# Attention layer on one core: the values' token sums on GpSimd, the products in another order, the heads' softmax apart, and another order at the end

## The chip, the cores and the metric

The kernel runs on one core of a Trainium2 chip. The metric is the device time of one launch in microseconds; the median of the runs shown is 1431.13 us (three runs, 1431.04 to 1432.65). One further execution was taken by the hardware profiler: it took 1434.23 us, of which the span of the instructions is 1432.5 us.

The engines are named as the profile names them: PE is TensorE (matmul; PEld its weight loads), DVE is VectorE, ACT is ScalarE, POOL is GpSimd, SP is SyncE, which here only issues DMAs.

## The reference, cut to what matters

Two layers on 512 tokens of width 1024, all in float32: a dilated window attention with 8 heads in three groups (windows 128, 512, 2048 with dilations 1, 4, 16), an mLSTM mixer, and a SwiGLU after each. Only the attention layer and the first lines of the SwiGLU behind it bear on the change:

```python
def dilated_attention_mixer(xn, positions, w_in, w_out):
    proj = (xn @ w_in).reshape(B, S, N_GROUPS, 3, ATTN_HEADS, ATTN_HEAD_DIM)
    ...
    for g, (window, dilation) in enumerate(DIL_CONFIGS):
        q = apply_partial_rope(proj[:, :, g, 0], positions) * scale
        k = apply_partial_rope(proj[:, :, g, 1], positions)
        v = proj[:, :, g, 2]
        o, lse = dilated_window_attention(q, k, v, window, dilation)
        ...
    wts = jax.nn.softmax(jnp.stack(lses), axis=0)
    o = jnp.einsum('gbsh,gbshd->bshd', wts.astype(xn.dtype), jnp.stack(outs))
    return o.reshape(B, S, ATTN_WIDTH) @ w_out

h = h + dilated_attention_mixer(rms_norm(h, attn_norm), ...)
h = h + swiglu(rms_norm(h, ffn_norm), ...)
```

## The kernel before, in words

**Split operands.** Each float32 operand of a matmul is split into a high half that TensorE takes exactly and the rest, the low half, and three matmuls are added: high times high, low times high, high times low. A chunk of weights (128 x 1024) comes by a DMA that SP issues (`load_chunk`, L201, three buffers), its high half is a copy on ScalarE (`split_chunk`, L209) and its low half a subtraction on DVE (L210). An operand is complete when L210 has run. Of the names, `a0g1k_k0` is the first half along the contraction of the weights for pair 0, group 1, keys; `_w`, `_h`, `_l` are the chunk and its halves. Activations are split in the same way (L224, L225; L228 where a gain is applied: `n_h`, `n_l`).

**Pairs of heads.** `project_pair` makes queries and keys of one pair of heads for the three groups, six projections of 48 matmuls. Each ends in one of three PSUM banks (`acc`); DVE multiplies it by the cosines out of the bank (L765 or L767) and shuffles the rotated part out (L556), after which the bank is free, then `rotate` finishes the rotation in SBUF (L559, L562, L564).

**Values.** For pair 0 the projections run beside the making of normalized tokens `xn` (`normalize`, L800: one DVE operation that multiplies h by the gain and by the broadcast inverse norm `xrbc`) and of four sums S1 to S4 of blocks of them (`sums_a`, `sums_b`, L830 to L839 with the splits L818 and L819). `values_phase` then makes the values of all heads with a Strassen scheme: seven products P1 to P7 for each of three units, with sums and differences of weight blocks made on DVE (L868) and split by L209 and L210. `prepare_values` runs two products ahead of `multiply_values`.

**Attention of a pair.** `attention_pair` makes scores (PE L633), their exponentials (DVE and ACT), and then `rest`: `joint` (the exchange between groups, PE L669), for each head `weigh` (DVE L701, L704) and `transposes` (a DVE transpose L710 to `pB` and four GpSimd-issued DMAs of it to DRAM, `pD`, L713), then for both heads `bring` (a GpSimd-issued DMA from `pD` into `pT`, L718). `values` multiplies `pT` with the values (PE L728, L733). `load_values` brings the values of a pair from DRAM (GpSimd-issued DMAs L595, L598).

**What sets the order.** The program is written out by hand and each engine takes its instructions in one order, which the scheduler derives from it and from what waits for what. `defer(n, fn)` puts work n steps (half projections) behind the present one, `advance` counts the steps, `run` closes a piece of PE work off by a fence, and `fenced` puts matmuls behind the last fence. The attention work of pair p runs so beside the projections of pair p + 1, at the steps of `RUN_AT`.

**The end.** The last pair has no projections beside it. The output projection (`awo`, four chunks of 256 columns, 24 matmuls for each half of the contraction) fills its place: `out_part(c, whl, ch, ks)` multiplies chunk c. Chunks 0 to 2 wait in PSUM for the last heads and are then added to h (L995); chunk 3 comes last, in one piece of 48 matmuls (`out_project(..., first=3)`). Then the squares of h are summed (`n1ssum`, L366) and the first SwiGLU starts with its weights `f0j`.

Of the kernel before, what the change touches and what calls it, by code (L numbers as in the profile page):

```python
# [17 lines left out]
P = 128  # L18
# [16 lines left out]
SCORES0_AT = 4  # L35
RUN_AT = (3, 5, 10)
STACK_AT = (9, 11, 15, 17)
# [34 lines left out]
def tile_hybrid_dilated_attn_mlstm(  # L72
# [296 lines left out]
    with ExitStack() as actx:  # L369
# [203 lines left out]
        def attention_pair(pr, qks):  # L573
# [13 lines left out]

            def load_values(last=False):
                for g in range(3):
                    t = (ap.tile([P, TB, 256], F32, tag="qk", name="%sv%d" % (nm, g), bufs=6) if last else  # L590
                         ap2.tile([P, TB, 256], F32, tag="v%d" % g, name="%sv%d" % (nm, g)))
                    src = vD[g][pr // 2][:, pr % 2 * 256:(pr % 2 + 1) * 256]
                    if g == 0:
                        for c in range(4):
                            nc.gpsimd.dma_start(t[R * c:R * (c + 1)],  # L595
                                                src.rearrange("(c b j) f -> c j b f", c=4, b=TB)[c])
# [151 lines left out]
            return (lambda: (places(), scores0(*qks[0])), lambda: scores12(*qks[1:]), rest, values, load_values)  # L748

        def project_pair(pr, qks, then=None):  # L750
# [3 lines left out]
            for g in range(3):  # L754
# [3 lines left out]
                for part in range(2):  # L758
# [26 lines left out]
                    if pr == 0 and 1 <= g and not first:  # L785
                        step = 2 * (g - 1) + part
                        (lambda: normalize(range(4)), lambda: normalize(range(4, 8)), sums_a, sums_b)[step]()
# [8 lines left out]
        def normalize(ks):  # L796
            for k in ks:
                if k % 2 == 0:
                    xn.append(place(("w2", "w3", "st0", "st1")[k // 2], "xn%d" % (k // 2)))
                nc.vector.scalar_tensor_tensor(xn[k // 2][:, k % 2], h[k], col("attn", k), rbc,  # L800
                                               op0=ALU.mult, op1=ALU.mult)

# [11 lines left out]

        def split_sum(name, raw):
            S[name] = ([heads_s[:, 2 * (int(name[1]) - 1) + i] for i in range(2)] if name in ("S1", "S2") else
                       [place("s%d" % (2 * (name == "S4") + i), name + "hl"[i], (P, 4, HALF), F32R) for i in range(2)])
            nc.scalar.activation(S[name][0], raw, AF.Copy)  # L818
            nc.vector.tensor_tensor(S[name][1], raw, S[name][0].bitcast(F32), op=ALU.subtract)  # L819
        sums = {}  # L820

        def two(fn):
            for i in range(2):
                fn(i, slice(2 * i, 2 * i + 2))

        def sums_a():
            nonlocal heads_s
            heads_s = ap.tile([P, 4, 4, HALF], F32R, tag="heads", name="S12")
            raw = sums["chain"] = place("w4", "Sr", (P, 4, HALF))
            two(lambda i, ks: nc.vector.tensor_tensor(raw[:, ks], xblock(1, 0, i), xblock(1, 1, i), op=ALU.add))  # L830
            split_sum("S1", raw)
            two(lambda i, ks: nc.vector.tensor_tensor(raw[:, ks], raw[:, ks], xblock(0, 0, i), op=ALU.subtract))
            split_sum("S2", raw)

        def sums_b():
            raw, r3 = sums["chain"], place("w5", "S3r", (P, 4, HALF))
            two(lambda i, ks: nc.vector.tensor_tensor(r3[:, ks], xblock(0, 0, i), xblock(1, 0, i), op=ALU.subtract))
            split_sum("S3", r3)
            two(lambda i, ks: nc.vector.tensor_tensor(raw[:, ks], xblock(0, 1, i), raw[:, ks], op=ALU.subtract))  # L839
            split_sum("S4", raw)  # L840
        heads_s = None
# [49 lines left out]
        def values_phase():  # L891
# [59 lines left out]
            for hf in range(2):  # L951
                load_block(0, "W12", hf)
            for hf in range(2):
                load_block(0, "W22", hf)
# [16 lines left out]
        def follow(todo, following=None):  # L971
            scores12_, rest, values, _ = todo[1:]

            def last():
                run(lambda: values(0), lambda: values(1))
                following[4]()
            defer(RUN_AT[0], lambda: run(scores12_))
            defer(RUN_AT[1], lambda: run(rest))
            if following is not None:
                defer(RUN_AT[2], last)  # L980
        for pr in range(1, HEADS // 2):
            qks = []
# [4 lines left out]
        _, last_scores, last_rest, last_values, load_last = todo  # L987
        out_first = split_chunk(weight_chunk(attn_w_out[0], 0, 0, 4, "awo0_k0"))
        pair = x_tiles("ao")
# [8 lines left out]
        def out_project(pairs, w2d, nk, name, first=0, end=KC // 2):  # L998
            for c in range(first, end):
# [3 lines left out]
        assert not later  # L1003
        acc = [[acc_tile("awo0_%d" % m) for m in range(2)],
               [ps.tile([P, 512], F32, tag="s", name="awo1_%d" % m, bufs=2) for m in range(2)],
               [acc_tile("awo2_0"), ps.tile([P, 512], F32, tag="t", name="awo2_1", bufs=1)]]

        def out_part(c, whl, ch, ks=None, last=False):
            for m in range(2):
                with fenced():  # L1010
                    multiply(acc[c][m], whl, pair, ch, m, KC, ks)
                if last:
                    add_to_h(c)(m, acc[c][m])

# [6 lines left out]
        load_last(True)  # L1021
        out_part(2, out_weights(2, 0), 0)
# [8 lines left out]
        for k in range(2, 4):  # L1031
            for c in range(3):
                out_part(c, whl[c], 1, (k,), k == 3)
# [1056 lines left out]
```

## Time and profile before

| | |
|---|---|
| median of three runs | 1431.13 us (1431.04 to 1432.65) |
| the profiled execution | 1434.23 us, span 1432.5 us |
| busy: PE, DVE, ACT, POOL | 97%, 80%, 50%, 11% of the span |
| mean granted clock of TensorE | 0.987 |
| attention layer, to the first matmul of f0j | 533.5 us |

The page cuts the span into forty slices of about 36 us, a digit each for the busy share in tenths; PE shows 9 in all slices but a few, and those are in the attention layer, at the start and at the end. In the list of waits each row names the engine and line that waited, what it waited for (engine or DMA, the tile and its line), the sum in us, the number of times and the longest. A row of the timeline holds the start, the duration, engine, line and operation, the tiles written and read, and in brackets how long the engine sat idle before it and what ended that.

### The profile page before, as it was taken

The page shows a single profiled execution, that of the slowest core. Times are in us where ns is not written, and L with a number is a line of the kernel's source. Part 1 is how long each engine was busy: PE and PEld are TensorE (multiplying, and loading weights), DVE is VectorE, ACT ScalarE, POOL GpSimd, SP SyncE. Part 2 cuts the span into 40 slices and gives each one's busy share as a digit, 9 for nine tenths or more (in the row PEclk, how much of TensorE's full clock was granted, in tenths as well). Part 3 has the DMA queues.
Part 4 walks back from the last instruction along what each step waited for, and adds up shares of the span by engine and source line. Part 5 has one row for each costly group of instructions (what it writes and reads, how often), then busy time and mean ns, then how long its engine had stood idle before and what let it go on. Part 6 is the DMA issues. An engine that isn't in the chain of part 4 may idle for free. (4 is left out here: it accounts for less than half of the span.)

```text
span 1432.5 us, 21509 instructions
## 1 busy us (share of the span) xinstructions
PE 1387.5 (97%) x8284; PEld 1233.9 (86%) x8284; DVE 1139.4 (80%) x1922; ACT 710.0 (50%) x1159; POOL 158.2 (11%) x229
## 2 busy tenths in 40 slices
PE   9889999999999699999999999999999999999997
PEld 7678888887877588999999998888888899999886
DVE  7997757768596559977887889988767987887887
ACT  6245544232232244444557654687444544557854
POOL 1000000201110101000001101022201240001203
PEclk9999999999999899999999999999999999999999
DMA  6425533726345426533335363323433563335963
GB/s 210 128 74 176 177 103 118 214 88 196 120 128 159 142 86 160 149 118 119 94 104 157 94 172 105 89 69 109 118 103 102 136 208 122 98 95 149 194 162 106
DMA packets 135231, 188.10 MB, mean 131 GB/s; under 512 B 8469, under 2 KB 100181, under 8 KB 135129
## 3 DMA queue, kind: packets, MB, share of 16 engines
q1 hardware_dynamic: 115136, 134.17, 30.2%
q0 software_dynamic: 18336, 51.43, 15.2%
q8 instruction: 65, 1.06, 0.3%
q10 hardware_dynamic: 1656, 1.12, 0.2%
q14 instruction: 38, 0.30, 0.1%
HBM read 164.68 MB, written 19.92 MB: 129 GB/s over the span
## 5 line engine op out<-in xcount | busy, mean ns | idle before, releaser
L1393 POOL DMA_DIRECT2D f1T<-in_ffn_w_out_dram x15 | 17.8, 1196 | 208.8 <-DMA f1P_2w_w<-in_ffn_w_out_dram 136.0
L1368 POOL DMA_DIRECT2D f0S<-in_ffn_w_out_dram x10 | 8.7, 894 | 247.4 <-DVE f0hid L1285 172.9
L1925 POOL DMA_DIRECT2D hD<-hB x32 | 21.7, 697 | 68.5 <-DVE hB L1922 68.5
L240 PE MATMUL awo<-ao_h,awo_k_h 128*128 128x512 f32 x64 | 25.9, 404 | 0.0
L240 PE MATMUL awo<-ao_h,awo_k_l 128*128 128x512 f32 x64 | 25.6, 403 | 0.2 <-DVE awo_k_l L210 0.2
L240 PE MATMUL awo<-ao_l,awo_k_h 128*128 128x512 f32 x64 | 25.6, 400 | 0.0
L240 PE MATMUL mo<-n_h,mo_k_l 128*128 128x512 f32 x64 | 25.3, 395 | 0.0
L240 PE MATMUL mo<-n_h,mo_k_h 128*128 128x512 f32 x64 | 25.2, 394 | 0.0
L240 PE MATMUL mo<-n_l,mo_k_h 128*128 128x512 f32 x64 | 25.1, 393 | 0.0
L240 PE MATMUL mwo<-yo_l,mwo_k_h 128*128 128x512 f32 x64 | 25.1, 393 | 0.0
L240 PE MATMUL mqk<-n_h,mqk_k_h 128*128 128x512 f32 x64 | 25.1, 392 | 0.0
L240 PE MATMUL mqk<-n_l,mqk_k_h 128*128 128x512 f32 x64 | 25.1, 392 | 0.0
L240 PE MATMUL f1j<-n_h,f1j_h 128*128 128x512 f32 x64 | 25.0, 391 | 0.0
L240 PE MATMUL f0j<-n_h,f0j_h 128*128 128x512 f32 x64 | 25.0, 391 | 0.0
L240 PE MATMUL mwo<-yo_h,mwo_k_l 128*128 128x512 f32 x64 | 25.0, 391 | 0.0
L240 PE MATMUL mqk<-n_h,mqk_k_l 128*128 128x512 f32 x64 | 25.0, 390 | 0.0
L240 PE MATMUL f0j<-n_h,f0j_l 128*128 128x512 f32 x64 | 24.9, 390 | 0.0
L240 PE MATMUL f1j<-n_h,f1j_l 128*128 128x512 f32 x64 | 24.9, 390 | 0.0
L240 PE MATMUL f0j<-n_l,f0j_h 128*128 128x512 f32 x64 | 24.9, 389 | 0.0
L240 PE MATMUL f1j<-n_l,f1j_h 128*128 128x512 f32 x64 | 24.9, 389 | 0.0
L240 PE MATMUL mwo<-yo_h,mwo_k_h 128*128 128x512 f32 x64 | 24.8, 391 | 0.0
L210 DVE TENSOR_TENSOR v1P_l<-v1W,v1P_h 128x1024 fp32r<-128x1024 f32 x14 | 17.1, 1224 | 9.5 <-ACT v1P_h L209 9.5
(2518 smaller groups left out, 5700.0 us busy)
## 6 DMA issues: line engine op xcount, KB each, us to landing
f0j_w<-in_ffn_w_in_dram SPq DMA_DIRECT2D x17, 512.0 KB, 5.7
f1j_w<-in_ffn_w_in_dram SPq DMA_DIRECT2D x17, 512.0 KB, 6.1
f1T<-in_ffn_w_out_dram POOLq DMA_DIRECT2D x15, 512.0 KB, 7.9
f0hid<-in_ffn_w_in_dram SPq DMA_DIRECT2D x9, 512.0 KB, 5.2
f1hid<-in_ffn_w_in_dram SPq DMA_DIRECT2D x9, 512.0 KB, 5.0
v0W<-in_attn_w_in_dram SPq DMA_DIRECT2D x8, 512.0 KB, 4.7
v1W<-in_attn_w_in_dram SPq DMA_DIRECT2D x8, 512.0 KB, 5.1
v2W<-in_attn_w_in_dram SPq DMA_DIRECT2D x8, 512.0 KB, 4.1
```

The lines of the kernel that those rows point to most:

```text
L210: nc.vector.tensor_tensor(lo[:, :n], raw[:, :n], hi[:, :n].bitcast(F32), op=ALU.subtract)
L240: nc.tensor.matmul(acc, whl[a][:, k, m * P:(m + 1) * P], pairs[b][kk], start=(kk == 0 and (a, b) == SPLITS[0]), stop=(kk == nk - 1 and (a, ...
L1368: nc.gpsimd.dma_start(t, src[1][:, ks], accum_op=ALU.add)
L1393: nc.gpsimd.dma_start(view(to), weight_rows(hk * UNITS + u, n), accum_op=ALU.add)
L1925: nc.gpsimd.dma_start(hD[k // 4].rearrange("(b i) x -> i b x", i=R)[:, :, c0:c0 + R], t[R * a_:R * (a_ + 1)])
```

## The change

- `normalize` becomes two operations: a scaled copy of h on ScalarE (L804) and a product with `xrbc` on GpSimd, in place (L805). All eight tokens' blocks are written in one step, where before there were two steps.
- The sums S1 to S4 are made on GpSimd (L828). The order is S1 and S3, then the split of S1, S2, the split of S3, the split of S2, S4, and the split of S4 in `values_phase`.
- The seven products run in the order P1, P5, P2, P6, P7, P3, P4.
- `rest` is cut in three: `joint` with the first head's weights and transposes; the first head's `bring` with the second head's weights and transposes; the second head's `bring`. They stand at steps 5, 7 and 9. The next pair's values are loaded group by group, at steps 10, 11 and 12.
- At the end the last scores come first, then the first halves of output chunks 0 and 3; chunk 3's first half is added to h at once. The three pieces of `rest` stand between the output chunks, whose parts come in another order, and of chunk 3 only the second half is left for the end.

```diff
-RUN_AT = (3, 5, 10)
+RUN_AT = (3, (5, 7, 9), 10, (10, 11, 12))
...
-            def rest():
+            def first_rest():
                 joint()
-                for i in range(2):
-                    weigh(i)
-                    transposes(i)
-                for i in range(2):
-                    bring(i)
+                weigh(0)
+                transposes(0)
+
+            def second_rest():
+                bring(0)
+                weigh(1)
+                transposes(1)
...
-                nc.vector.scalar_tensor_tensor(xn[k // 2][:, k % 2], h[k], col("attn", k), rbc,
-                                               op0=ALU.mult, op1=ALU.mult)
+                t = xn[k // 2][:, k % 2]
+                nc.scalar.activation(t, h[k], AF.Copy, scale=col("attn", k))
+                nc.gpsimd.tensor_tensor(t, t, rbc, op=ALU.mult)
...
+        def raw_sum(name, x, y, op):
...
+            for i in range(2):
+                nc.gpsimd.tensor_tensor(piece_of(name, i), piece_of(x, i), piece_of(y, i), op=op)
...
+        def raw_sums():
...
+            raw_sum("S1", of(1, 0), of(1, 1), ALU.add)
+            raw_sum("S3", of(0, 0), of(1, 0), ALU.subtract)
+
+        def more_sums():
+            split_sum("S1")
+            raw_sum("S2", "S1", of(0, 0), ALU.subtract)
+            split_sum("S3")
+
+        def last_sums():
+            split_sum("S2")
+            raw_sum("S4", of(0, 1), "S2", ALU.subtract)
...
-        ORDER = ("P1", "P5", "P6", "P2", "P7", "P3", "P4")
+        ORDER = ("P1", "P5", "P2", "P6", "P7", "P3", "P4")
...
         run(lambda: before[3](0, head_split), lambda: before[3](1, head_split))
-        out_part(0, out_first, 0)
         run(last_scores)
+        acc[0] = [acc_tile("awo0_%d" % m) for m in range(2)]
+        out_part(0, out_weights(0, 0), 0)
         load_last(True)
+        acc[3] = two_of("o", 3, 2)
+        whl = {3: out_weights(3, 0)}
+        for m in range(2):
...
+            add_part(3, m)
+        run(last_rest[0])
+        acc[1] = two_of("s", 1, 2)
+        out_part(1, out_weights(1, 0), 0)
+        last_rest[1]()
...
         out_part(2, out_weights(2, 0), 0)
-        run(last_rest)
-        out_part(1, out_weights(1, 0), 0)
         whl = [out_weights(c, 1) for c in range(3)]
-        for i in (0, 2):
-            out_part(i, whl[i], 1, (0, 1))
+        last_rest[2]()
+        for c in range(2):
+            out_part(c, whl[c], 1, (0, 1))
         run(lambda: last_values(0, head_split))
-        out_part(1, whl[1], 1, (0, 1))
+        out_part(2, whl[2], 1, (0, 1))
+        for c in range(2):
+            out_part(c, whl[c], 1, (2,))
         run(lambda: last_values(1, head_split))
...
-    out_project(pair, attn_w_out[0], KC, "awo", first=3)
+    whl = split_chunk(weight_chunk(attn_w_out[0], 1, 3 * 256, 4, "awo3_k1"))
+    for m in range(2):
...
+        add_to_h(3)(m, acc)
```

The change moves instructions at three places that the prediction speaks of. The first is DVE in pair 0, between the rotation of group 0 and the low half of the first key weights of group 1 (`a0g1k_k_l`); `xn_...` are normalized tokens. Before:

```order
L767 TENSOR_TENSOR a0g_q<-a0g1q_456,ropc 128x512
L556 STREAM_SHUFFLE rot<-a0g1q_456 32x512
L767 TENSOR_TENSOR a0g_q<-a0g1q_457,ropc 128x512
L556 STREAM_SHUFFLE rot<-a0g1q_457 32x512
L800 SCALAR_TENSOR_TENSOR xn_518<-h_97,cols,xrbc 128x512
L559 TENSOR_TENSOR rot<-rot,rops 32x1024
L800 SCALAR_TENSOR_TENSOR xn_521<-h_98,cols,xrbc 128x512
L564 TENSOR_TENSOR a0g_q<-a0g_q,rot 32x1024
L800 SCALAR_TENSOR_TENSOR xn_521<-h_99,cols,xrbc 128x512
L210 TENSOR_TENSOR a0g1k_k_l<-a0g1k_k_w,a0g1k_k_h 128x1024
```

The same place after the change:

```order
L770 TENSOR_TENSOR a0g_q<-a0g1q_456,ropc 128x512
L556 STREAM_SHUFFLE rot<-a0g1q_456 32x512
L210 TENSOR_TENSOR a0g1k_k_l<-a0g1k_k_w,a0g1k_k_h 128x1024
L770 TENSOR_TENSOR a0g_q<-a0g1q_457,ropc 128x512
L556 STREAM_SHUFFLE rot<-a0g1q_457 32x512
L129 COPY cols<-rowsT 128x72
L559 TENSOR_TENSOR rot<-rot,rops 32x1024
```

The low half now stands behind one evacuation and its shuffle instead of two, and the normalized tokens and the end of the rotation no longer stand ahead of it.

The second place is GpSimd's queue at the last pair, where `a3pD` are the transposed weights on their way to DRAM and `a3pT` the way back. Before:

```order
L598 DMA a3v_3611<-vD_376 128x4x256
L598 DMA a3v_3613<-vD_378 128x4x256
L713 DMA a3pD<-a3pB 32x4x480 x8
L718 DMA a3pT<-a3pD 128x1920 x2
L1368 DMA f0S_0_6339<-in_ffn_w_out_dram 128x512
```

After:

```order
L598 DMA a3v_3615<-vD_376 128x4x256
L598 DMA a3v_3617<-vD_378 128x4x256
L713 DMA a3pD<-a3pB 32x4x480 x5
L718 DMA a3pT<-a3pD 128x1920
L713 DMA a3pD<-a3pB 32x4x480 x3
L718 DMA a3pT<-a3pD 128x1920
```

The first head's way back now stands ahead of three of the second head's four ways out.

The third place is DVE at the change from the attention layer to the first SwiGLU, where `h_...` are the sums with the output chunks, `n1ssum` the sum of squares, `n_l_...` low halves of the scaled tokens and `f0j_00_l` the low half of the first SwiGLU weights. Before:

```order
L995 TENSOR_TENSOR h_101<-awo_1_3487,h_101 128x512
L366 TENSOR_TENSOR n1ssum<-n1ssum,n1sq 128x512
L210 TENSOR_TENSOR awo_k_l<-awo_k_w,awo_k_h 128x1024
L366 TENSOR_TENSOR n1ssum<-n1ssum,n1sq 128x512
L210 TENSOR_TENSOR f0j_00_l<-f0j_00_w,f0j_00_h 128x1024
L366 TENSOR_TENSOR n1ssum<-n1ssum,n1sq 128x512
L228 SCALAR_TENSOR_TENSOR n_l_3952<-h_96,cols,n_h_3951 128x512
L366 TENSOR_TENSOR n1ssum<-n1ssum,n1sq 128x512
```

After, the last rows of that stretch:

```order
L1009 TENSOR_TENSOR h_103<-awo_1_3943,h_103 128x512
L366 TENSOR_TENSOR n1ssum<-n1ssum,n1sq 128x512
L228 SCALAR_TENSOR_TENSOR n_l_3966<-h_98,cols,n_h_3965 128x512
L366 TENSOR_TENSOR n1ssum<-n1ssum,n1sq 128x512
L228 SCALAR_TENSOR_TENSOR n_l_3966<-h_99,cols,n_h_3965 128x512
L366 TENSOR_TENSOR n1ssum<-n1ssum,n1sq 128x512
L228 SCALAR_TENSOR_TENSOR n_l_3968<-h_100,cols,n_h_3967 128x512
L228 SCALAR_TENSOR_TENSOR n_l_3968<-h_101,cols,n_h_3967 128x512
L228 SCALAR_TENSOR_TENSOR n_l_3970<-h_102,cols,n_h_3969 128x512
L228 SCALAR_TENSOR_TENSOR n_l_3970<-h_103,cols,n_h_3969 128x512
L210 TENSOR_TENSOR f0j_00_l<-f0j_00_w,f0j_00_h 128x1024
```

The low half of f0j now stands behind all sums of h, all sums of squares and all eight low halves of the tokens; before, it stood behind the first six sums of h and two sums of squares.

More of the change, by code (lines that the diff above doesn't have):

```diff
@@ L586, in places, with load_values @@
                 p12.extend(t[:, 7:] for t in p)
-            def load_values(last=False):
-                for g in range(3):
+            def load_values(last=False, groups=range(3)):
+                for g in groups:
                     t = (ap.tile([P, TB, 256], F32, tag="qk", name="%sv%d" % (nm, g), bufs=6) if last else
@@ L816, in split_sum @@
+        def split_sum(name):
             S[name] = ([heads_s[:, 2 * (int(name[1]) - 1) + i] for i in range(2)] if name in ("S1", "S2") else
                        [place("s%d" % (2 * (name == "S4") + i), name + "hl"[i], (P, 4, HALF), F32R) for i in range(2)])
[L818 to L824, printed above, removed]
@@ L826, in sums_a @@
-        def sums_a():
+            hi, lo = S[name]
+            nc.scalar.activation(hi, raws_of[name], AF.Copy)
+            nc.vector.tensor_tensor(lo, raws_of[name], hi.bitcast(F32), op=ALU.subtract)
+        of = lambda t, kh: lambda i: xblock(t, kh, i)
+        def raw_sums():
             nonlocal heads_s
             heads_s = ap.tile([P, 4, 4, HALF], F32R, tag="heads", name="S12")
[L829 to L833, printed above, removed]
@@ L1003, in tile_hybrid_dilated_attn_mlstm, with out_part @@
         assert not later
[L1004 to L1008, printed above, removed]
+        two_of = lambda tag, c, bufs: [ps.tile([P, 512], F32, tag=tag, name="awo%d_%d" % (c, m), bufs=bufs)
+                                       for m in range(2)]
+        acc = {}
+        def out_part(c, whl, ch, ks=None, add=None):
             for m in range(2):
@@ L1011, in out_part, with add_part @@
                     multiply(acc[c][m], whl, pair, ch, m, KC, ks)
-                if last:
-                    add_to_h(c)(m, acc[c][m])
+                if add is not None:
+                    add(c, m)
+        def add_part(c, m):
+            add_to_h(c)(m, acc[c][m])
         def out_weights(c, ch):
@@ L1037, in tile_hybrid_dilated_attn_mlstm @@
         add_square(k)
-    out_project(pair, attn_w_out[0], KC, "awo", first=3)
+    whl = split_chunk(weight_chunk(attn_w_out[0], 1, 3 * 256, 4, "awo3_k1"))
+    for m in range(2):
+        acc = acc_tile("awo3_%d" % m)
+        with fenced():
+            for k in range(4):
+                for a, b in SPLITS:
+                    nc.tensor.matmul(acc, whl[a][:, k, m * P:(m + 1) * P], pair[b][4 + k],
+                                     start=(k == 0 and (a, b) == SPLITS[0]),
+                                     stop=(k == 3 and (a, b) == SPLITS[-1]))
+        add_to_h(3)(m, acc)
+    advance()
     for k in range(KC - 2, KC):
```

39 lines of the change are left out of this document (24 added, 15 removed).

## The prediction

> **What bounds the kernel now.** I read the page's busy shares first, then TensorE's waits, then tables of short windows around each wait, then the timeline there.
>
> ```profile
> PE 1387.5 (97%) x8284; PEld 1233.9 (86%) x8284; DVE 1139.4 (80%) x1922; ACT 710.0 (50%) x1159; POOL 158.2 (11%) x229
> PE a3o L728 <- DMA a3pT<-a3pD: 10.5, 1, 10.5
> PE a0g1k L240 <- DVE a0g1k_k_l L210: 4.6, 1, 4.6
> PE v0p L944 <- ACT v0P_h L209: 3.2, 1, 3.2
> PE a3g2k L240 <- DVE rot L556: 3.1, 1, 3.1
> PE a3xps L669 <- DVE a3ex L664: 2.2, 1, 2.2
> PE a1g2q L240 <- DVE a1g2q_k_l L210: 2.2, 1, 2.2
> ```
>
> TensorE is busy 1387.5 of 1432.5 us, so all its waits together are 45 us. The change leaves the number of matmuls as it is. It can therefore win only what these waits cost, and lose only by new ones; the largest six all lie in the attention layer, the first 533 us. A wait costs more than its length, as the windows show:
>
> ```profile
> 40.00:60.00 20.00, 14.95 (x58) 11.51 (x57) 19.54 (x29) 2.89 (x3) 0.00 (x0) 0.83 0.28 88
> 60.00:80.00 20.00, 20.00 (x90) 16.57 (x89) 19.43 (x28) 8.49 (x10) 0.00 (x0) 1.00 0.49 151
> 80.00:100.00 20.00, 15.74 (x61) 12.11 (x60) 20.00 (x26) 8.55 (x13) 0.00 (x0) 0.86 0.24 77
> ```
>
> The columns are busy time and count of PE, PEld, DVE, ACT and POOL, then the granted clock, the DMA share and GB/s. A full window holds 90 matmuls (0.222 us each). The first holds 58: 32 missing, 7.1 us, of which the wait at a0g1k is 4.6 and a small one 0.5. The other 2.0 us are matmuls at a low clock (0.83 in the mean) behind the wait. The third holds 61: 6.4 us lost, by the waits of 3.2 and 1.0 and again about 2 us of low clock. So I add 2 us to a wait of over 2 us. DVE is 97 to 100% busy from 40 to 100 us: there, what DVE does ahead of a needed operand sets the time.
>
> **1. The normalized tokens and their sums on GpSimd.** These are DVE's rows on the way to the first wait, then the wait:
>
> ```profile
> L800 DVE SCALAR_TENSOR_TENSOR xn<-h,cols,xrbc 128x512 f32<-128x512 f32 x8 | 5.6, 731 | 0.0
> L830 DVE TENSOR_TENSOR Sr<-xn,xn 128x512 f32<-128x512 f32 x2 | 1.3, 672 | 0.0
> 30.96 0.68 DVE L341 COPY xrbc<-xbc 128x512 f32<-128x512 f32 x1
> 39.47 2.33 DVE L559 TENSOR_TENSOR rot<-rot,rops 32x1024 f32<-32x1024 f32 x2
> 41.73 1.27 DVE L562 TENSOR_TENSOR a0g_q<-a0g_q,rot 32x512 f32<-32x512 f32 x2
> 42.93 1.28 DVE L562 TENSOR_TENSOR a0g_k<-a0g_k,rot 32x512 f32<-32x512 f32 x2
> 51.42 1.20 DVE L210 TENSOR_TENSOR a0g1k_k_l<-a0g1k_k_w,a0g1k_k_h 128x1024 fp32r<-128x1024 f32 x1
> 52.68 0.80 PE L240 MATMUL a0g1k<-xa_h,a0g1k_k_l 128*128 128x512 f32 x1 [4.57 <-DVE a0g1k_k_l L210]
> ```
>
> DVE loses eight products (5.6 us) and eight sums of two SBUF inputs (two in 1.3 us, so 0.6 to 0.67 each, about 4.9 us): 10.5 us. In the new order the low half of a0g1k also stands ahead of a second evacuation. If GpSimd cost DVE nothing, that L210 would end about 45.9 us (from 38.8, where the rotations then begin, one L800 of 0.7 before them being gone: four L562 and two L559 are 4.7, one evacuation with its shuffle 1.2, L210 1.2). The matmuls ahead of the wait end at 52.68 - 4.57 = 48.1, so it would be gone.
>
> Does GpSimd cost DVE nothing? At the end of the program stand four GpSimd products of the same form (128x512, two SBUF inputs):
>
> ```profile
> L1988 POOL TENSOR_TENSOR ht<-ht,gbc x4: 1300/1524/2347, 1413.0 to 1418.3; 128x512 f32<-128x512 f32 x4
> 1413.87 0.44 DVE L1993 TENSOR_TENSOR fpre<-fss 128x1 f32<-128x1 f32 x1
> 1414.23 1.21 DVE L210 TENSOR_TENSOR f1P_4w_l<-f1T,f1P_4w_h 128x1024 fp32r<-128x1024 f32 x1
> 1415.43 1.72 DVE L1339 TENSOR_TENSOR f1P<-f1hid,f1P 128x512 fp32r<-128x512 f32 x1
> L1339 DVE TENSOR_TENSOR f0P<-f0hid,f0P x25: 676/684/686, 745.3 to 858.3; 128x512 fp32r<-128x512 f32 x25
> ```
>
> The last row of the fence is not of this place, and shows what L1339 takes elsewhere: 0.68. Here, with GpSimd at work, it took 1.72, so 1.04 more. One GpSimd product takes 1.30 alone and 2.35 at worst, which is 1.05 more, about DVE's 1.2 of L210 that lay beside it. I read this as turns: a GpSimd product and a DVE operation with two SBUF inputs do not run at once, and neither gets two turns in a row.
>
> The Trainium skill ("SBUF — State Buffer", section "Who interferes with whom") calls these the shared pair of ports, held for a whole instruction, and lets a DVE instruction with one SBUF input pass; the rows agree with the holding. The Trainium skill ("GPSIMD Engine Reference", section 4.1) speaks against the move outright: element-wise work belongs on VectorE, GpSimd being some 2 times slower; 1.30 against 0.67 bears that out, and by it the move gains nothing.
>
> With turns: twelve GpSimd operations are ready from about 32 us, behind the copy of xrbc. Four or five of them pass beside DVE's evacuations from PSUM, to 38.8. Then stand six DVE operations with two SBUF inputs, and each waits for a GpSimd one: 4.7 + 5 x 1.30 + 0.4 = 11.6, to 50.4; evacuation and shuffle to 51.3 to 51.6, L210 to 52.5. Before it ended at 52.6. So the first wait stays: the 5.6 us taken off DVE are paid back in turns.
>
> Then the second place:
>
> ```profile
> 92.41 3.48 DVE L868 TENSOR_TENSOR v0W<-v0W,v0W 128x1024 f32<-128x1024 f32 x3
> 94.82 1.22 PE L944 MATMUL v0p<-v0P_h,S 128*128 128x512 f32 x2 [3.22 <-ACT v0P_h L209]
> 97.08 0.80 PE L944 MATMUL v0p<-v0P_l,S 128*128 128x512 f32 x1 [1.04 <-DVE v0P_l L210]
> ```
>
> P5 waits for the difference of weights (L868), which waits only for its turn on DVE. Taken off ahead of it: 10.5 us. Added: 6.9 in the turns above; for the five later GpSimd operations up to 1.30 each, taken at half, 3.3; and a new row of waits, about 1.5, since ScalarE's halves of the sums (S12, S3, S4) now wait for GpSimd, in a queue in which the halves of the weights a0g1k_k1, a0g2q and a0g2k stand behind them, and S4's low half on DVE waits for ScalarE. That is 11.7: P5 comes 1.2 later, say **+1.2 us**. Bounds: no turns, and both waits go with their low clock, 4.6 + 0.5 + 2.0 + 3.2 + 1.0 + 2.0 = 13.3 us faster; a full turn for each of the sixteen, 16 x 1.30 - 10.5 = 10.3 us slower. I stand near the middle because the rows at 1414 show turns, and because half of DVE's rows there read PSUM or have their operands apart. ScalarE's eight new scalings (about 0.6 each) lie in idle time: it is busy 2.89 us of 20 from 40 to 60.
>
> **2. P2 ahead of P6.** P2 needs no difference, so P6's is made behind it. TensorE has no wait at P6 that the list of before shows: 0, and at most 1.0, as at v0P_l, comes back.
>
> **3. The heads' softmax apart.** Pairs 1 to 3 wait at g2q for a low half (2.2 us in pair 1, no more in the others), with DVE full; the same work stands ahead of it in both orders, so these stay. The wait at a3g2k is of another kind:
>
> ```profile
> 418.00:430.00 12.00, 10.30 (x49) 8.41 (x48) 12.00 (x24) 3.56 (x9) 5.68 (x12) 1.00 0.90 246
> 430.00:442.00 12.00, 12.00 (x54) 9.68 (x52) 4.25 (x12) 2.73 (x11) 1.16 (x2) 1.00 0.97 289
> 427.65 0.55 POOL L718 DMA_DIRECT2D a2pT<-a2pD  x1 [4.01 <-DMA a2pD<-a2pB]
> 428.20 2.21 POOL L595 DMA_DIRECT2D a3v<-vD  x4
> 429.55 0.37 SPq L201 DMA_DIRECT2D a3g2k_k_w<-in_attn_w_in_dram  x1
> 441.65 1.06 ACT L209 ACTIVATE a3g2k_k_h<-a3g2k_k_w 128x1024 fp32r<-128x1024 f32 x1 [6.52 <-DMA a3g2k_k_w<-in_attn_w_in_dram]
> 445.26 0.50 PE L240 MATMUL a3g2k<-xa_h,a3g2k_k_h 128*128 128x512 f32 x1 [3.14 <-DVE rot L556]
> ```
>
> The weight chunk was issued at 429.55 and used at 441.65, 12.1 us on, with the DMA engines 0.90 to 0.97 busy: the second pT and four loads of values had been issued just ahead. Now the second head's transposes come about 3.5 us later, so these are issued behind the chunk. TensorE ran dry 3.1 us before 445.26; a chunk landing 3.1 us sooner ends the wait: **-5.1 us** (3.1 and 2.0 of low clock). Bounds: 0, if the pD traffic alone fills the engines; I take the full gain, since 12.1 us need only become 9.0. The second pT of pairs 0 to 2 lands later, but their products have 6 us to spare by my reading.
>
> **4. The end in another order.**
>
> ```profile
> 478.70 0.49 PE L669 MATMUL a3xps<-a3ex,acst 128*128 128x128 f32 x2 [2.17 <-DVE a3ex L664]
> 487.41 2.22 POOL L713 DMA_DIRECT2D a3pD<-a3pB  x4 [16.17 <-DVE a3pB L710]
> 494.61 0.56 POOL L718 DMA_DIRECT2D a3pT<-a3pD  x1
> 502.71 3.35 PE L728 MATMUL a3o<-a3pT,a3v 128*128 128x128 f32 x14 [10.49 <-DMA a3pT<-a3pD]
> 519.43 2.05 DVE L995 TENSOR_TENSOR h<-awo,h 128x512 f32<-128x512 f32 x3 [3.48 <-PE awo L240]
> 526.66 1.22 DVE L210 TENSOR_TENSOR f0j_l<-f0j_w,f0j_h 128x1024 fp32r<-128x1024 f32 x1
> 533.51 0.39 PE L240 MATMUL f0j<-n_h,f0j_h 128*128 128x512 f32 x1
> ```
>
> The scores now come first and 48 output matmuls (10.9 us) cover the softmax, so the wait at a3xps goes and the exchange comes 2.5 us sooner. The first pT now stands behind one pD of the second head instead of four, which is another 1.7 us at most: issue at 490.5 to 492 instead of 494.6. It landed 8.1 us on before; I take 5.5 to 8.1. So a3o starts between 496 and 500, at 498 say, **-4.7**, and TensorE waits some 5 us there.
>
> What follows has less cover. Of chunk 3's 48 matmuls 24 now stand ahead, so only 24 lie between the last sums of h and the first FFN. On DVE the low half of f0j's first weights, done by 527.9 (8.4 us after the first sum) before, now stands behind every sum of h, seven sums of squares and eight low halves of the normalized tokens. From the first sum: eight sums of h and seven of squares at 0.61, two L210 at 1.14, eight low halves at 0.66 (rows' durations less the 0.07 by which neighbours overlap: 526.66 + 1.22 ends at 527.9, and L800's form took 5.6 for eight): 9.2 + 2.3 + 5.3 = 16.8 us. TensorE comes to the first matmul that reads it 15 + 24 + 8 = 47 matmuls, 10.4 us, after the first sum, and waits about 6; with 2 of low clock it passes that point at 18.8. Before, the same point (f0j's ninth matmul, 8 x 0.222 past 533.51) lay at 15.9. That is **+2.9** against the -4.7: **-1.8 us**, from +0.6 (pT lands after 8.1) to -4.
>
> **Sum.** +1.2 + 0 - 5.1 - 1.8 = -5.7. The profiled execution took 1434.23 (span 1432.5 and 1.7 around it), so it would take 1428.5; the median of the runs shown is 1431.13, 3.1 below, and gives 1425.4. I round up to **1426**, as each step of 3 and 4 leans on a landing time.
>
> **Rivals.**
> (a) GpSimd and DVE hardly meet. For it: only eight DVE operations were beside GpSimd in the trace. Against: 1.72 for 0.68. Both early waits go: 1431.1 - 13.3 - 5.1 - 1.8 = 1411, and half of it 1419.
> (b) The moved traffic does not free the chunk. For it: the engines were 0.90 busy before pT too. Then 1426 + 5.1 = 1431, no change.
> (c) Slower: GpSimd becomes DVE's bottleneck between 32 and 92 us. Every one of sixteen operations holds DVE for 1.30, DVE comes 10.3 later to L868, and P5 waits 13 instead of 3: 1431.1 + 10.3 - 5.1 - 1.8 = 1434.5, and 1439.6 with (b). It decides from 13 full turns of the 16 on (17.4 us paid, 6.9 net, which eats what 3 and 4 bring). For it: DVE is 97 to 100% busy there, so every turn counts, and ScalarE's queue waits for GpSimd as well. Against: evacuations read PSUM. The Trainium skill ("GPSIMD Engine Reference", section 2.1) adds some 6 us at the first call of a freshly loaded GpSimd routine; no trace here shows that, and it would push the same way.
> (d) It does not do what it says: DVE gets its time back only to wait for GpSimd. That is my own step 1.
>
> **Chances.** Forecast 0.43 (own range 1421 to 1430), (a) 0.12, (b) 0.13, (c) 0.32. I give (c) this much because the two gains rest on landing times, while its cost lies on a full engine. A measurement of this kernel can tell about 0.2%, 2.9 us, from no change. Faster by more: 0.47 (eight tenths of the forecast's 0.43, and (a)); within: 0.2 ((b), the forecast's end); slower: 0.33 ((c), a little of (b)). Range: down to 1412, at the end of (a), and up to 1438, within (c) with (b).
>
> **What would show it.** Right: the wait at a0g1k still 3 to 5 us with L559 and L562 stretched by about 1.3 each beside GpSimd rows; P5 waiting 3 to 6; no wait at a3g2k nor a3xps; a3o waiting about 5; a new wait of about 6 at f0j's first matmul that reads a low half. Wrong: L562 at 0.6 beside GpSimd, and no wait at a0g1k (then (a)); a wait over 8 at P5 (then (c)); a chunk of a3g2k that takes 12 us again (then (b)).

## The result, and the profile after

The changed kernel takes 1432.57 us (median of 12 runs, 1430.48 to 1433.88), the kernel before 1431.09 us (12 runs, 1428.83 to 1433.71): a ratio of 1.0007, 95% interval 0.9999 to 1.0016. The forecast was 1426 us: no change was measured, where a gain of 5 us was the likeliest case. The profiled execution of the changed kernel took 1432.88 us, its span is 1431.1 us.

The page's busy shares, then TensorE's waits of the changed kernel (the total in us, times, the longest):

```profile
PE 1387.1 (97%) x8284; PEld 1234.1 (86%) x8284; DVE 1138.5 (80%) x1908; ACT 714.4 (50%) x1167; POOL 185.7 (13%) x245
PE a3o L728 <- DMA a3pT<-a3pD: 7.6, 1, 7.6
PE a0g1k L240 <- DVE rot L556: 5.2, 1, 5.2
PE v0p L956 <- ACT v0P_h L209: 3.8, 1, 3.8
PE f0j L240 <- DVE f0j_l L210: 2.7, 1, 2.7
PE n1ss L1102 <- DVE n1ssum L366: 2.4, 1, 2.4
PE a1g2q L240 <- DVE a1g2q_k_l L210: 2.2, 1, 2.2
...
PE a0g2k L240 <- DVE rot L556: 1.6, 1, 1.6
```

Two waits of before are not in this list any more, a3g2k (3.1) and a3xps (2.2). a3o is shorter by 2.9. Against that, a0g1k and P5 (v0p) are longer by 0.6 each, and three are new: two at the start of the first SwiGLU (5.1 together) and one at a0g2k. P5's second wait (1.0) is gone too, and one of 0.9 stands new at the product behind it. The sum of the waits hardly moved, and the time with it.

**Pair 0.** The timeline of DVE and the last rows of GpSimd's products there, with TensorE's wait:

```profile
38.75 4.58 DVE L559 TENSOR_TENSOR rot<-rot,rops 32x1024 f32<-32x1024 f32 x2
43.26 3.47 DVE L562 TENSOR_TENSOR a0g_q<-a0g_q,rot 32x512 f32<-32x512 f32 x2
46.66 3.41 DVE L562 TENSOR_TENSOR a0g_k<-a0g_k,rot 32x512 f32<-32x512 f32 x2
51.23 1.19 DVE L210 TENSOR_TENSOR a0g1k_k_l<-a0g1k_k_w,a0g1k_k_h 128x1024 fp32r<-128x1024 f32 x1
31.63 12.86 POOL L805 TENSOR_TENSOR xn<-xn,xrbc 128x512 f32<-128x512 f32 x8 [17.62 <-DVE xrbc L341]
44.44 3.41 POOL L828 TENSOR_TENSOR S1r<-xn,xn 128x512 f32<-128x512 f32 x2
51.37 0.79 PE L240 MATMUL a0g1k<-xa_h,a0g1k_k_h 128*128 128x512 f32 x1 [5.22 <-DVE rot L556]
52.48 0.80 PE L240 MATMUL a0g1k<-xa_h,a0g1k_k_l 128*128 128x512 f32 x1
```

The six operations L559 and L562 took 11.5 us, against 4.9 before: 6.6 more, 1.1 for each. GpSimd's sums take 1.70 each beside them instead of 1.30. These are the turns. The low half of a0g1k ends at 52.4, as forecast (52.5), and the wait stays. But it is not the low half that TensorE stops for first: the late evacuation holds a PSUM bank until its shuffle (L556) ends at 51.3, which before was done at 45.5. TensorE reads the low half at 52.48, before at 52.68.

Further on, DVE stands idle, which it did not before (rows of DVE with the idle time before them, one row of ScalarE, and P5):

```profile
59.96 1.23 DVE L210 TENSOR_TENSOR a0g2q_k_l<-a0g2q_k_w,a0g2q_k_h 128x1024 fp32r<-128x1024 f32 x1 [1.62 <-ACT a0g2q_k_h L209]
66.02 1.06 ACT L834 ACTIVATE S<-S1r 128x1024 fp32r<-128x1024 f32 x1 [6.09 <-POOL S1r L828]
68.06 1.23 DVE L210 TENSOR_TENSOR a0g2k_k_l<-a0g2k_k_w,a0g2k_k_h 128x1024 fp32r<-128x1024 f32 x1 [1.97 <-ACT a0g2k_k_h L209]
77.19 1.23 DVE L835 TENSOR_TENSOR S4l<-S1r,S4h 128x1024 fp32r<-128x1024 f32 x1 [2.28 <-ACT S4h L834]
97.38 1.22 PE L956 MATMUL v0p<-v0P_h,S 128*128 128x512 f32 x2 [3.78 <-ACT v0P_h L209]
```

DVE waits for ScalarE three times, 5.9 us of idle time on the engine that sets when P5 starts. Twice (1.97 and 2.28) ScalarE itself was held up by GpSimd's sums, for 6.09 and 5.29 us. The first time (1.62) it was not: the run below with the sums on DVE has 1.51 at the same place. P5 starts at 97.4 instead of 94.8, and the second unit of the values 2.6 us later than before (134.2, before 131.6).

**The last projection and the end.** Transfers and engines around a3g2k, then from the last pT to the first SwiGLU:

```profile
437.25 0.56 POOL L718 DMA_DIRECT2D a2pT<-a2pD  x1 [7.39 <-DMA a2pD<-a2pB]
432.20 0.37 SPq L201 DMA_DIRECT2D a3g2k_k_w<-in_attn_w_in_dram  x1
438.42 1.06 ACT L209 ACTIVATE a3g2k_k_h<-a3g2k_k_w 128x1024 fp32r<-128x1024 f32 x1 [0.64 <-DMA a3g2k_k_w<-in_attn_w_in_dram]
490.27 0.56 POOL L718 DMA_DIRECT2D a3pT<-a3pD  x1 [1.63 <-DMA a3pD<-a3pB]
498.26 3.33 PE L728 MATMUL a3o<-a3pT,a3v 128*128 128x128 f32 x14 [7.55 <-DMA a3pT<-a3pD]
515.33 2.06 DVE L1009 TENSOR_TENSOR h<-awo,h 128x512 f32<-128x512 f32 x3 [0.83 <-PE awo L240]
528.43 1.05 PE L1102 MATMUL n1ss<-ones,n1ssum 128*128 128x1 f32 x8 [2.39 <-DVE n1ssum L366]
530.95 2.35 DVE L210 TENSOR_TENSOR f0j_l<-f0j_w,f0j_h 128x1024 fp32r<-128x1024 f32 x2
532.21 0.79 PE L240 MATMUL f0j<-n_h,f0j_l 128*128 128x512 f32 x1 [2.73 <-DVE f0j_l L210]
```

The weight chunk of a3g2k is used 6.2 us after its issue (438.42 - 432.20), where before it took 12.1: the second pT and the values are issued behind it. From the start of the first sum of h to the first matmul that reads f0j's low half pass 16.9 us (532.21 - 515.33), as the sum of DVE's rows had it (16.8).

### The profile page after: what moved, and what is told of

It reads as the page before. It is cut to its first block, busy times and chain, and to the rows that moved or that the text cites. A ratio compares the mean times of both kernels' runs of the same rounds, so it can differ in the third digit from the quotient of the medians.

```text
span 1431.1 us, 21521 instructions
## 1 busy us (share of the span) xinstructions
PE 1387.1 (97%) x8284; PEld 1234.1 (86%) x8284; DVE 1138.5 (80%) x1908; ACT 714.4 (50%) x1167; POOL 185.7 (13%) x245
## 5 line engine op out<-in xcount | busy, mean ns | idle before, releaser
L210 DVE TENSOR_TENSOR v2P_l<-v2W,v2P_h 128x1024 fp32r<-128x1024 f32 x14 | 17.1, 1222 | 9.6 <-ACT v2P_h L209 9.6
L210 DVE TENSOR_TENSOR v1P_l<-v1W,v1P_h 128x1024 fp32r<-128x1024 f32 x14 | 17.1, 1223 | 9.6 <-ACT v1P_h L209 9.6
L210 DVE TENSOR_TENSOR v0P_l<-v0W,v0P_h 128x1024 fp32r<-128x1024 f32 x14 | 16.9, 1217 | 8.8 <-ACT v0P_h L209 8.8
L559 DVE TENSOR_TENSOR rot<-rot,sinn 32x1024 f32<-32x1024 f32 x18 | 21.7, 1207 | 0.1
```

Of the source, the lines that this page charges most:

```text
L210: nc.vector.tensor_tensor(lo[:, :n], raw[:, :n], hi[:, :n].bitcast(F32), op=ALU.subtract)
L559: nc.vector.tensor_tensor(sh, sh, sines.unsqueeze(1).to_broadcast([R, 2, SEQ]), op=ALU.mult)
```

## The experiments

The ratios are to the kernel before in the same session, since its median moves by 1 us from one session to the next (1431.09 to 1432.46). "v1c" is the start of the second unit of the values in the profiled execution, a point behind all the work of pair 0; before it lies at 131.6. It differs between traces of the same work: the three runs below with parts two to four and without the first have it at 130.7, 131.2 and 132.4.

**The four parts, each alone.**

Tokens and sums on GpSimd:

```diff
+                nc.scalar.activation(t, h[k], AF.Copy, scale=col("attn", k))
+                nc.gpsimd.tensor_tensor(t, t, rbc, op=ALU.mult)
...
+                nc.gpsimd.tensor_tensor(piece_of(name, i), piece_of(x, i), piece_of(y, i), op=op)
```

> The kernel before with only the first part of the change: normalized tokens and the four sums on GpSimd; products, softmax and end as before. My theory (turns on a shared way into SBUF): DVE's rows L559 and L562 between 38 and 50 us take about 1.1 us more each, the wait at a0g1k stays at 4 to 5.5 us, P5 starts about 2.5 us later than before (near 97.4 instead of 94.8), and the time is 2 to 3 us above before. Rival (the step relieves DVE, and what was lost was lost elsewhere): no change or faster, and P5 not later.

Measured: ratio 1.0017 (1.0008 to 1.0025), 2.4 us slower; v1c at 135.2; P5 at 98.1. L559 and L562 are as long as in the changed kernel. The first part costs time, by itself.

The softmax of the heads apart:

```diff
-RUN_AT = (3, 5, 10)
+RUN_AT = (3, (5, 7, 9), 10, (10, 11, 12))
```

> The kernel before with only the softmax of the two heads apart (steps 5, 7, 9, values group by group); the old tokens, products and end. My theory: the second chunk of a3g2k is issued ahead of the second pT, the wait of 3.1 us at a3g2k and its low clock go, 4 to 5 us faster. Rival: that wait is a matter of the one traced execution, the runs mostly don't have it, and the gain is 0 to 2 us. Second rival: the low clock that the wait at a1g2q then meets eats 1.6 us of it.

Measured: ratio 0.9964 (0.9952 to 0.9976), 5.1 us faster, with no wait at a3g2k. The first theory holds, but the size has two sources. The four other kernels that leave this part as it was show the wait at 1.3 to 2.8 us. From the first matmul of a3g0q to the first of a2o, a stretch with the wait in it, they and the kernel before take 75.8 to 79.3 us, 77.7 in the mean; this run takes 74.25. So 3.5 us come from there on average, and 5.0 only against the one trace of before. The rest comes at the last pair, whose `rest` is cut in three here too:

```profile
490.01 0.56 POOL L718 DMA_DIRECT2D a3pT<-a3pD  x1 [1.77 <-DMA a3pD<-a3pB]
```

Counted from the start of the last matmul of a2o, a3o starts after 39.5 us, in the five others after 40.5 to 41.1. The first pT was not issued sooner (33.0 us after that matmul, before 32.9), since it waits for its own pD; it landed after 6.3 us instead of 7.6 to 8.2.

The end in another order, with `rest` cut in its three pieces but run as one at step 5:

```diff
-            defer(RUN_AT[1], lambda: run(rest))
+            defer(RUN_AT[1], lambda: run(lambda: [fn() for fn in rest]))
...
(and the new end)
```

> The kernel before with only the new end of the attention layer. My theory: the wait at a3xps goes and a3o starts about 2 to 4 us sooner from the end of a2o, but the first SwiGLU waits about 5 us for n1ssum and f0j's low half; in sum between 1 us faster and 2 us slower. Rival (the end is worth what the prediction gave it): 2 us or more faster.

Measured: ratio 0.9989 (0.9978 to 1.0001), some 1.6 us faster, a little more than I expected at best. But the two parts are not apart in this run. GpSimd and ScalarE around a3g2k:

```profile
430.89 0.56 POOL L718 DMA_DIRECT2D a2pT<-a2pD  x1 [5.84 <-DMA a2pD<-a2pB]
434.80 1.04 ACT L209 ACTIVATE a3g2k_k_h<-a3g2k_k_w 128x1024 fp32r<-128x1024 f32 x1
```

The cut of `rest` alone puts the first head's `bring` ahead of the second head's transfers, so the second pT comes behind the weight chunk here too, and the wait at a3g2k is gone. The stretch from a3g0q to a2o takes 74.2 us here as well. This run holds the gain of the third part as well as the fourth. Behind it the new end is slower: from the last matmul of a2o to the first of the mLSTM 438.1 us, with the old end 437.1 to 437.6 in five traces. What the end is worth shows better between two kernels that both lack that wait, below.

The order of products:

```diff
-        ORDER = ("P1", "P5", "P6", "P2", "P7", "P3", "P4")
+        ORDER = ("P1", "P5", "P2", "P6", "P7", "P3", "P4")
```

> The kernel before with only the order of products P1, P5, P2, P6, P7, P3, P4. My theory: the wait of 1.0 us for P5's low half goes, the wait of 3.2 us for its high half stays; between 0 and 1.5 us faster. Rival: P2 only moves the same DVE work, no change at all at v1c's start (131.6 us).

Measured: ratio 0.9999 (0.9989 to 1.0009), v1c at 131.6 to the tenth. The rival holds: the wait of 1.0 us at P5's low half is gone, and a new one of 0.9 at the following product takes its place.

**Parts two to four without the first.** The tokens and sums as before, everything else as in the changed kernel:

```diff
-                nc.scalar.activation(t, h[k], AF.Copy, scale=col("attn", k))
-                nc.gpsimd.tensor_tensor(t, t, rbc, op=ALU.mult)
+                nc.vector.scalar_tensor_tensor(xn[k // 2][:, k % 2], h[k], col("attn", k), rbc,
+                                               op0=ALU.mult, op1=ALU.mult)
...
(and the sums on nc.vector)
```

> The changed kernel with tokens and sums as before, on DVE: parts two to four of the change without the first. My theory: the first part cost 2.6 us, so this is 2 to 3.5 us faster than the changed kernel and 1 to 4 us faster than before. Rival (GpSimd's share was free): as the changed kernel, within 1 us.

Measured: ratio 0.9979 (0.9969 to 0.9989), 3.0 us faster than before. Against the changed kernel's 1.0007 the first part costs about 4 us. Against the heads' softmax alone (0.9964) the new end and order cost 2.1 us by the ratios, but the two intervals overlap. The traces point the same way: from the last matmul of a2o to the first of the mLSTM it is 435.5 us with the old end and the heads apart (457.0 to 892.5) and 437.7 with the new one (455.8 to 893.5). So the end as it stands brings nothing, and is likely a loss.

**f0j's low half.** The first weights of the SwiGLU are split ahead of the normalized tokens in program order:

```diff
+    early = [split_chunk(weight_chunk(ffn_w_in[0], 0, half * D_FF, 4, "f0j0_%d0" % half)) for half in range(1)]
     pair, rbc, _, hook = norm("ffn", 0, "n1", ssum)
```

> The changed kernel with f0j's first weights split ahead of the normalized tokens, so that their low half stands behind one sum of squares on DVE. My theory: the waits of 2.4 and 2.7 us at the start of the first SwiGLU and the low clock behind them go for the larger part, 3 to 6 us faster than the changed kernel. Rival (DVE's chain of sums and low halves is itself the bound, whatever stands first): under 1.5 us faster, with the wait now at a low half of the tokens.

Measured: ratio 0.9951 (0.9935 to 0.9966), 7 us faster than before, and by the two ratios 8 us faster than the changed kernel. The timeline of DVE, and TensorE's first matmul that reads the low half:

```profile
513.46 2.06 DVE L1009 TENSOR_TENSOR h<-awo,h 128x512 f32<-128x512 f32 x3 [0.82 <-PE awo L240]
518.95 1.22 DVE L210 TENSOR_TENSOR f0j_l<-f0j_w,f0j_h 128x1024 fp32r<-128x1024 f32 x1
523.03 0.39 PE L240 MATMUL f0j<-n_h,f0j_l 128*128 128x512 f32 x1
```

The gain is larger than the 3 to 6 us that I expected. The low half is done 6.7 us after the start of the first sum of h instead of 16.8, TensorE reads it without a wait, and the low clock behind the two waits goes too. From f0j's first matmul to the first of the mLSTM it is 366.3 us (522.1 to 888.4) instead of 373.3. The same 24 matmuls of chunk 3 are enough cover, if that one row stands early. So the place in DVE's order was the cause, not the length of its chain.

Both of the last two:

```diff
(parts two to four of the change, and the early split; tokens and sums on nc.vector)
```

> Both: tokens and sums on DVE as before, and f0j's first weights split early. If the two losses are independent, 5 to 9 us faster than the changed kernel, 4 to 8 faster than before (1423 to 1427 us). If they are not, no more than the better of the two alone.

Measured: 1422.19 us, ratio 0.9931 (0.9916 to 0.9946), 9.9 us faster than before, more than the 4 to 8 expected. Against the changed kernel that is 10.9 us by the ratios, and the two runs before give 4 and 8: the two losses add up within the noise, and this version beats both kernels. TensorE's waits in it:

```profile
PE a3o L728 <- DMA a3pT<-a3pD: 6.9, 1, 6.9
PE a0g1k L240 <- DVE a0g1k_k_l L210: 4.6, 1, 4.6
PE v0p L947 <- ACT v0P_h L209: 3.2, 1, 3.2
```

**What GpSimd costs DVE.** Two constant writes in place of each of the sixteen GpSimd operations; this leaves the products and the sums of the tokens out.

```diff
-                nc.gpsimd.tensor_tensor(t, t, rbc, op=ALU.mult)
+                nc.gpsimd.memset(t, 1.0)
+                nc.gpsimd.memset(t, 1.0)
...
(the same for the sums)
```

> The changed kernel with each of the sixteen GpSimd operations replaced by two writes of a constant to the same place (about 1.1 us together), which read nothing from SBUF; so the products and sums of the tokens are left out. My theory (what costs DVE its time is GpSimd's reading beside it): L559 and L562 go back to 1.13 and 0.6 us, the wait at a0g1k is under 1 us, P5 starts without a wait of over 1.5 us, and it is 8 to 14 us faster than the changed kernel. Rival (any GpSimd work on SBUF holds DVE): L562 still near 1.7 us each and no more than 4 us faster.

Measured: ratio 0.9961 (0.9946 to 0.9976). DVE's rows in the run in which GpSimd writes and does not read:

```profile
45.35 2.33 DVE L559 TENSOR_TENSOR rot<-rot,rops 32x1024 f32<-32x1024 f32 x2
47.61 1.27 DVE L562 TENSOR_TENSOR a0g_q<-a0g_q,rot 32x512 f32<-32x512 f32 x2
```

They are back at 1.2 and 0.6 each, and 0.3 is left of the wait at a0g1k. But GpSimd was done with the first writes by 43 us, before L559 began, so this run shows what the absence of GpSimd's work is worth and not that a writing GpSimd beside these rows would be harmless. The gain is smaller than I expected: 6.6 us from the changed kernel by the ratios, not 8 to 14. P5 still waits 1.7, and a new wait of 3.1 stands at a0g0q, for a high half on ScalarE, whose order moved.

**Tokens or sums?** Only the eight token products on GpSimd, the sums on DVE; and the other way round:

```diff
(first) +                nc.gpsimd.tensor_tensor(t, t, rbc, op=ALU.mult)
(second) +                nc.gpsimd.tensor_tensor(piece_of(name, i), piece_of(x, i), piece_of(y, i), op=op)
```

> The kernel before with only the eight token products on ScalarE and GpSimd; the four sums stay on DVE. It parts the 2.4 us that the first part costs. My theory: the turns (L559 and L562 are 6.6 us longer together) about pay for the 5.6 us taken off DVE, the rest of the loss is DVE idle behind sums made on GpSimd; so here v1c starts within 1.5 us of the kernel before (131.6), and P5 within 1.5 of 94.8. Rival (the turns are the whole loss): v1c 2.5 us or more later.

> The kernel before with only the four sums on GpSimd; the token products stay on DVE. My theory: DVE loses some 5 us of sums and gains 4 to 6 us of idle time, since ScalarE's halves of the weights stand behind its halves of the sums and those wait for GpSimd; v1c starts 1 to 3 us later than before. Rival (the loss is all in the turns with the token products): v1c at 131.6 or earlier.

Measured: tokens alone 0.9990 (0.9978 to 1.0003), v1c at 130.6; sums alone 1.0029 (1.0017 to 1.0041), v1c at 135.3, which is 3.7 us later and more than the 1 to 3 expected. The loss is in the sums. (With the sums the order of their splits moves too, as in the change; that order with the sums on DVE was not run.) The tokens alone, timeline:

```profile
31.94 11.29 POOL L802 TENSOR_TENSOR xn<-xn,xrbc 128x512 f32<-128x512 f32 x8 [17.55 <-ACT xn L801]
35.33 1.77 DVE L838 TENSOR_TENSOR S3r<-xn 128x512 f32<-128x512 f32 x1 [1.25 <-POOL xn L802]
45.37 1.28 DVE L562 TENSOR_TENSOR a0g_q<-a0g_q,rot 32x512 f32<-32x512 f32 x2
93.45 0.94 PE L945 MATMUL v0p<-v0P_h,S 128*128 128x512 f32 x2 [4.03 <-ACT v0P_h L209]
```

GpSimd is done at 43.2, before L562 begins, and most of its work lay beside DVE's evacuations. So the turns that I had put down to the tokens come for the larger part from the sums that follow them. Of the wait at a0g1k 1.1 us are left instead of 4.6, but 1.5 stand new at a0g1q, for an evacuation behind a sum on DVE that itself waits for a token (the second row). And at v1c 1 us arrives, which is no more than the spread of that point: DVE stays 100% busy from 60 to 100 us, and P5 now waits 4.0 and 1.3. The wait moved along the queue of the full engine.

The sums alone, timeline:

```profile
57.44 5.91 POOL L824 TENSOR_TENSOR S1r<-xn,xn 128x512 f32<-128x512 f32 x2 [2.48 <-DVE xn L800]
58.61 1.21 DVE L210 TENSOR_TENSOR a0g2q_k_l<-a0g2q_k_w,a0g2q_k_h 128x1024 fp32r<-128x1024 f32 x1
59.75 1.20 DVE L831 TENSOR_TENSOR S3l<-S3r,S3h 128x1024 fp32r<-128x1024 f32 x1
63.38 1.06 ACT L830 ACTIVATE S<-S1r 128x1024 fp32r<-128x1024 f32 x1 [7.33 <-POOL S1r L824]
64.35 1.04 ACT L209 ACTIVATE a0g2q_k_h<-a0g2q_k_w 128x1024 fp32r<-128x1024 f32 x1
64.48 1.23 DVE L831 TENSOR_TENSOR S<-S1r,S 128x1024 fp32r<-128x1024 f32 x1 [3.52 <-ACT S L830]
```

Two sums take 5.9 us on GpSimd. ScalarE waits 7.3 us for them with the high half of a0g2q queued behind, and DVE waits 3.5 us for ScalarE. DVE was freed of these sums and stood idle for them. The two sums are not alike:

```profile
L824 POOL TENSOR_TENSOR S1r<-xn,xn x2: 1282/2977/4672, 57.4 to 62.1; 128x512 f32<-128x512 f32 x2
```

The first took 4.67 us, until 1.2 us after the last DVE row had ended at 60.95, and the DVE rows beside it kept their usual length; the second took 1.28 beside an idle DVE. So here GpSimd did not get every other turn: several DVE rows passed before it.

**What a3o waits for.** The last pair's transfers from ScalarE's queue, on top of the best version:

```diff
-                    nc.gpsimd.dma_start(d.rearrange("b j a x -> a j b x")[a],
+                    (nc.scalar if pr == HEADS // 2 - 1 else nc.gpsimd).dma_start(d.rearrange("b j a x -> a j b x")[a],
...
(the same for pT)
```

> Tokens and sums on DVE, f0j's first weights split early, and the last pair's pD and pT transfers issued from ScalarE's queue instead of GpSimd's (ScalarE is busy 2 of 20 us there). It parts what a3o waits for. If the issue of 0.55 us each on GpSimd and its descriptors are what is late, a3o's wait of 6.9 us falls by 2 to 4 us, to 1418 to 1420 us. If the transfers' own time on the DMA engines is (8 us from issue to use), it stays within 1 us of 1422.

Measured: 1422.53 us, ratio 0.9931 (0.9915 to 0.9947), no change. The issue of the first pT and the start of a3o, first from ScalarE's queue, then from GpSimd's (the best version):

```profile
487.32 0.35 ACTq L718 DMA_DIRECT2D a3pT<-a3pD  x1
495.96 3.33 PE L728 MATMUL a3o<-a3pT,a3v 128*128 128x128 f32 x14 [7.06 <-DMA a3pT<-a3pD]
486.98 0.56 POOL L718 DMA_DIRECT2D a3pT<-a3pD  x1 [1.51 <-DMA a3pD<-a3pB]
494.38 3.33 PE L728 MATMUL a3o<-a3pT,a3v 128*128 128x128 f32 x14 [6.86 <-DMA a3pT<-a3pD]
```

From the start of the last matmul of a2o the pT is issued after 29.8 us here and after 30.8 from GpSimd. It is used 8.6 us later instead of 7.4, so that a3o starts after 38.4 and 38.2 us. The issue came 1.0 us sooner and the use did not. So the queue that issues them is not what a3o waits for; what is left is the transfers themselves, to DRAM and back. What sets their length was not tested.

## Why the prediction was right or wrong

The measured time lies inside the range, at the case "no change" (0.2) rather than the forecast (0.43). That it does is owed to a range that reaches up to 1438: the gain of 5 us did not come. Point by point, in the terms of the sum:

- **Step 1, forecast +1.2; measured +2.4 (1.1 to 3.6) alone, about 4 within the change.** The mechanism was right: turns, the wait at a0g1k stays, P5 comes later. The turns in the first block were 6.6 against 6.9. That TensorE would stop there for a PSUM bank first was not foreseen, and changed little. What was mis-sized lies behind it. I priced the five later GpSimd operations at 3.3 of turns; only one row of DVE shows a full one (an L210 at 72.6 us took 2.30). And I priced the new row of waits, DVE behind ScalarE behind GpSimd, at 1.5; it was 4.3, and 1.6 of another kind came with it. I also blamed the tokens. The experiments show no loss by them (0.9990, 0.9978 to 1.0003), and the loss with the sums (1.0029). And "neither gets two turns in a row" is too strict: one GpSimd sum waited 3.4 us longer than alone (4.67).
- **Step 2, forecast 0; measured 0.9999.** Right, with a new wait of 0.9 in place of the old one of 1.0.
- **Step 3, forecast -5.1; measured -5.1 alone.** The mechanism was right: the chunk took 6.2 us instead of 12.1. That the size agrees to a tenth is luck in part. The wait is 1.3 to 3.1 us in the traces that have it, and its removal is worth 3.5 us in their mean; the rest came at the last pair, which the forecast had counted under step 4.
- **Step 4, forecast -1.8; by the traces +0.6 against the old end.** This is the step that failed most. Its loss was about right: +2.9 forecast, and from a3o to the mLSTM the four traces with this end and without the early split show 398.6 to 399.3 us instead of 396.1 to 396.7, 2.6 more in the mean. Its gain was not: -4.7 forecast, but a3o starts 38.4 to 39.3 us after a2o's last matmul instead of 40.5 to 41.1, 2.0 less. Of the terms, the exchange did come 2.3 us sooner. The 1.7 us for the shorter queue were wrong: pT waits 1.5 to 1.8 for its own pD to land, whatever stands in the queue. And pT landed 7.4 to 8.1 us after its issue in these four traces; I had taken the middle of 5.5 to 8.1. Two further runs with this end and the same order of transfers show 6.6 and 7.3. Why it varies is open.

The measured sizes add up: 2.4 to 4, less 3.5, and 0.6 give -0.5 to +1.1, and the ratio of 1.0007 is +1.0. Of the 6.7 us between that and the forecast's -5.7, 1.2 to 2.8 are step 1, 1.6 step 3 and 2.4 step 4.

Rival (a) is refuted by L562 in the trace. Rival (b) named the time that came, 1431, but not its cause: the chunk took 6.2 us. Rival (c) is refuted by its price: P5's wait was 3.8, not 13. Of the signs of being right one failed: a3o waited 7.6 us, not 5. The new wait of about 6 came in two pieces, 2.4 and 2.7.

## What to carry to other kernels

Taking work off a full engine brought nothing here where what stood next in that engine's queue came to wait for the work where it went: look for the engine in between (here ScalarE's halves, in order, behind GpSimd's sums). Work with a long lead (the tokens) could be moved without a loss, though no gain could be measured either; a link of a short chain (the sums) could not. When a block of matmuls that covered an engine's chain is cut, list that chain in the new order and look for the one row that TensorE needs first: moving that row was worth 8 us, more than any of the four parts of the change. And before a wait seen in one trace is priced, look at it in several: the wait at a3g2k was 3.1 us in the trace of before and 1.3 in another.

## What the runs showed of the hardware that I had not expected

- The low clock behind a wait is not a fixed price. The wait at a1g2q is 2.2 us in both traces; before, the matmuls behind it run on at 0.227 us each, after the change seven of them are 0.43 apart, while a2g2q, with the same wait, shows it the other way round. In each of the thirteen traces exactly one of these two waits is followed by 7 to 9 slow matmuls, and the stretch that holds both (a1g0q to a3g0q) takes 164.5 to 164.6 us in all of them. So the 2 us that I added to each wait is an amount that shifts from place to place between traces. After the change:

```profile
267.82 0.78 PE L240 MATMUL a1g2q<-xa_h,a1g2q_k_l 128*128 128x512 f32 x1 [2.17 <-DVE a1g2q_k_l L210]
268.40 0.63 PE L240 MATMUL a1g2q<-xa_h,a1g2q_k_h 128*128 128x512 f32 x1
```

- A GpSimd product of 128x512 is 1.30 us alone and as long beside DVE's evacuations out of PSUM (1.28 to 1.30 for four of the eight tokens). It took 2.27 beside L559, 1.7 in turns with L562, and once 4.67, with DVE rows of two SBUF inputs passing one after the other.
